# Trace of a batched matrix product: from casting loads with transposed B and a VectorE multiply-reduce to plain float32 loads with transposed A and TensorE matmuls

## The chip, the cores and the metric

The kernel runs on 1 core of one Trainium2 chip. Its time is the device time of one execution in microseconds (us). The span of a profile is some 2 us shorter than that time (718.2 against 720.2 us for the kernel before), because it covers the program's instructions alone. Ratios are computed as the mean time of one kernel's fast runs over that of the other's fast runs of the same rounds, so they are not quite the ratios of the medians quoted beside them.

## The reference

Eight pairs of 2176 x 2176 float32 matrices come in, eight numbers go out:

```python
def reference(a, b):                       # a, b: (8, 2176, 2176) float32
    prod = np.matmul(a, b)
    traces = np.diagonal(prod, axis1=1, axis2=2).sum(axis=-1)
    return traces.astype(np.float32)
```

Only the diagonal of each product is needed, so each trace is the sum over i and k of A[i,k] * B[k,i]. Each input number is used once. One of the two matrices must be transposed on the chip, so that A[i,k] and B[k,i] meet. (HBM is the memory that the inputs lie in, SBUF the memory on the chip that the engines read, PSUM the one that TensorE writes its results to; DMA engines carry the data from HBM to SBUF.) In this text a row tile is 128 rows of one matrix, 128 x 2176 numbers, 1.114 MB in float32. There are 17 in a matrix and 272 in all, 303.04 MB.

## The kernel before

The loads go through GpSimd and cast float32 to bf16 on the way. A whole A matrix lies in SBUF, double-buffered. Rows of B arrive in groups of two, their 128 x 128 blocks are transposed on TensorE into PSUM, and VectorE multiplies them with the matching part of A and sums.

```python
    a_pool = ctx.enter_context(tc.tile_pool(name="a_pool", bufs=2))
    b_pool = ctx.enter_context(tc.tile_pool(name="b_pool", bufs=5))
    # ... cut ...
    def load(dst, src, start, m):
        rows = src[start:start + P * m, :].rearrange("(p r) k -> p r k", r=m)
        nc.gpsimd.dma_start(out=dst, in_=rows)          # float32 -> bf16 on the way
    # ... cut: for each batch, for each group of B's rows ...
            load(b_tile[:, 0:m, :], b[bi], start, m)
            if not last:
                load_a(a_next, bi + 1, gi)
            for lo, hi in chunks:                        # 6, 6 and 5 blocks
                for s in range(m):
                    psum_tile = psum_pool.tile([P, 6, P], dt, tag="bT")
                    for u in range(lo, hi):
                        c0, step = slot_cols[u]
                        nc.tensor.transpose(
                            psum_tile[:, u - lo, :],
                            b_tile[:, s, c0:c0 + step * (P - 1) + 1:step],
                            identity,
                        )
                    nc.vector.tensor_tensor_reduce(      # product with A, and its sum
                        out=scratch[:, :w, :],
                        in0=a_all[:, lo:hi, start + s:start + s + m * (P - 1) + 1:m],
                        in1=psum_tile[:, :w, :],
                        # ... cut: multiply, add ...
                        accum_out=acc[:, col:col + 1],
                    )
```

Of the kernel before, what the change touches and what calls it, by code (L numbers as in the profile page):

```python
# [1 line left out]

# [5 lines left out]


def row_groups(n, p, rows):  # L10

    groups, at = [], 0
    while at < n:
        m = min(rows, (n - at) // p)
        groups.append((at, m))
        at += m * p
    return groups


@with_exitstack  # L20
def kernel(
    ctx: ExitStack,
    tc: tile.TileContext,
    a: bass.AP,
    b: bass.AP,
    out: bass.AP,
):
    nc = tc.nc
    P = 128
    BATCH, N, N2 = a.shape  # L30
    assert N == N2 and N % P == 0
    NT = N // P
    ROWS = 2
    CHUNKS = [(0, 6), (6, 12), (12, NT)]
    LAST_CHUNKS = [(0, 6), (6, 12), (12, 16), (16, NT)]

    dt = mybir.dt.bfloat16
    f32 = mybir.dt.float32

    const = ctx.enter_context(tc.tile_pool(name="const", bufs=1))  # L40
    a_pool = ctx.enter_context(tc.tile_pool(name="a_pool", bufs=2))
    b_pool = ctx.enter_context(tc.tile_pool(name="b_pool", bufs=5))
    psum_pool = ctx.enter_context(tc.tile_pool(name="psum", bufs=7, space=bass.MemoryType.PSUM))
    psum_small = ctx.enter_context(tc.tile_pool(name="psum_small", bufs=1, space=bass.MemoryType.PSUM))
    scratch_pool = ctx.enter_context(tc.tile_pool(name="scratch", bufs=2))
    acc_pool = ctx.enter_context(tc.tile_pool(name="acc", bufs=2))

    groups = row_groups(N, P, ROWS)

    slot_cols = [(start + r, m) for start, m in groups for r in range(m)]  # L50

    def load(dst, src, start, m):
        rows = src[start:start + P * m, :].rearrange("(p r) k -> p r k", r=m)
        nc.gpsimd.dma_start(out=dst, in_=rows)  # L54

    def load_a(a_all, bi, gi):
        start, m = groups[gi]
        slot = start // P
        load(a_all[:, slot:slot + m, :], a[bi], start, m)

    a_next = a_pool.tile([P, NT, N], dt, tag="a")
    for gi in range(len(groups)):
        load_a(a_next, 0, gi)

    identity = const.tile([P, P], dt, tag="identity")
    make_identity(nc, identity)
    ones = const.tile([P, 1], f32, tag="ones")
    nc.vector.memset(ones, 1.0)  # L68
    batch_accs = const.tile([P, BATCH], f32, tag="batch_accs")
    result_tile = const.tile([P, BATCH], f32, tag="result")  # L70

    for bi in range(BATCH):
        a_all = a_next
        last = bi == BATCH - 1
        b_groups = row_groups(N, P, 1 if last else ROWS)
        acc = acc_pool.tile([P, NT * len(LAST_CHUNKS)], f32, tag="acc")
        col = 0
        if not last:
            a_next = a_pool.tile([P, NT, N], dt, tag="a")

        for gi, (start, m) in enumerate(b_groups):
            b_tile = b_pool.tile([P, ROWS, N], dt, tag="b")
            pieces = last and gi >= len(b_groups) - 2
            chunks = LAST_CHUNKS if pieces else CHUNKS
            if pieces:
                for lo, hi in chunks:
                    nc.gpsimd.dma_start(  # L87
                        out=b_tile[:, 0, lo * P:hi * P],
                        in_=b[bi, start:start + P, lo * P:hi * P],
                    )  # L90
            else:
                load(b_tile[:, 0:m, :], b[bi], start, m)

            if not last:
                load_a(a_next, bi + 1, gi)

            for lo, hi in chunks:
                for s in range(m):
                    w = hi - lo
                    psum_tile = psum_pool.tile([P, 6, P], dt, tag="bT")  # L100
                    for u in range(lo, hi):
                        c0, step = slot_cols[u]
                        nc.tensor.transpose(  # L103
                            psum_tile[:, u - lo, :],
                            b_tile[:, s, c0:c0 + step * (P - 1) + 1:step],
                            identity,
                        )
                    scratch = scratch_pool.tile([P, 6, P], dt, tag="scr")
                    nc.vector.tensor_tensor_reduce(  # L109
                        out=scratch[:, :w, :],  # L110
                        in0=a_all[:, lo:hi, start + s:start + s + m * (P - 1) + 1:m],
                        in1=psum_tile[:, :w, :],
                        scale=1.0,
                        scalar=0.0,
                        op0=mybir.AluOpType.mult,
                        op1=mybir.AluOpType.add,
                        accum_out=acc[:, col:col + 1],
                    )
                    col += 1

        nc.vector.reduce_sum(  # L121
            out=batch_accs[:, bi:bi + 1], in_=acc[:, :col], axis=mybir.AxisListType.X
        )

    batch_psum = psum_small.tile([1, BATCH], f32, tag="bp")
    nc.tensor.matmul(batch_psum, ones, batch_accs, start=True, stop=True)  # L126
    nc.vector.tensor_copy(out=result_tile[:1, :BATCH], in_=batch_psum)  # L127

    nc.sync.dma_start(
        out=out.rearrange("(a b) -> a b", a=1),  # L130
        in_=result_tile[:1, :BATCH],
    )


# [1 line left out]
_INS = ['a', 'b']  # L136
_OUTS = [((8,), 'float32')]


# [23 lines left out]
```

## Time and profile before

| | before |
|---|---|
| time, median | 720.2 us |
| span of the profile | 718.2 us |
| read from HBM | 303.04 MB |
| load queue's share of the 16 DMA engines' span | 101.4% |
| VectorE, TensorE matmuls busy | 48%, 35% |
| instruction packets on the DMA engines | 18 |

The page of the profile before says first what each engine did. In the strips, each of 40 columns is one slice of the span, with the busy share in tenths or the GB/s that the DMA engines wrote. PE is TensorE's matmuls, PEld its weight loads, DVE VectorE, ACT ScalarE, POOL GpSimd, and SP SyncE. Then come the DMA queues with their packets, MB and share of the engines, and the chain of waits that ended last.

```profile
span 718.2 us, 6176 instructions
PE 248.2 (35%) x2314; PEld 228.3 (32%) x2314; DVE 347.1 (48%) x830; POOL 84.6 (12%) x164
...
DMA  8999999999999999999999999999999999999995
...
q0 software_dynamic: 22752, 151.53, 101.4%
q8 instruction: 18, 0.29, 0.1%
...
DMA 93%; issue 3%; PE 2%; DVE 1%; POOL 0%; POOLq 0%; ACTq 0%
```

The DMA engines are busy for 90% or more of every slice but the first and the last, and 93% of the chain is DMA. No compute engine is busy for half the span.

The table by stage for the kernel before gives, for each stretch of time, the busy us of each engine, the granted TensorE clock (as a share of full speed), the DMA share and the GB/s written:

```profile
core 0: us, PE busy (x) PEld busy (x) DVE busy (x) POOL busy (x), PEclk, DMA share, GB/s
20.00:600.00 580.00, 194.69 (x1802) 181.09 (x1802) 269.99 (x642) 62.58 (x118) 0.63 1.03 216
...
690.00:712.00 22.00, 13.56 (x151) 11.24 (x149) 21.74 (x51) 5.83 (x11) 0.78 0.95 180
```

bf16 is written and float32 is read, so 216 GB/s written are about 430 GB/s read. In the tail (the last line) VectorE is busy for 21.74 of 22 us, so there it is VectorE that ends last, on a backlog.

Two lines of the timeline before (start, us, engine, line, operation, tiles, how often, and the idle time before with its releaser) serve for the pace of TensorE: 34 transposes take 3.81 us.

```profile
646.84 3.54 PEld L103 LDWEIGHTS <-b_tile 128*128 128x128 bf16 x34 [6.79 <-DMA b_tile<-in_b_dram]
646.84 3.81 PE L103 MATMUL psum_tile<-identity,b_tile 128*128 128x128 bf16 x34 [6.53 <-DMA b_tile<-in_b_dram]
```

### The profile page before, as it was taken

What the parts mean: (1) busy time and instruction counts of PE and PEld (TensorE: products, weight loads), DVE (VectorE), ACT (ScalarE), POOL (GpSimd) and SP (SyncE); (2) the same over time, 40 slices, a digit from 0 to 9 for tenths busy, and PEclk for the clock granted to TensorE, in tenths of its full rate; (3) what the DMA queues carried; (4) which work ended last, traced back from release to release, by engine and by line L of the source; (5) the groups of instructions that cost most, each with busy time, mean ns of one, the idle gap of its engine ahead of it and who ended that gap; (6) DMA issues with size and microseconds to landing.
All of it is one profiled execution on the core that took longest, in us unless ns stands there. A gap on an engine that the chain in (4) does not pass through costs nothing.

```text
span 718.2 us, 6176 instructions
## 1 busy us (share of the span) xinstructions
PE 248.2 (35%) x2314; PEld 228.3 (32%) x2314; DVE 347.1 (48%) x830; POOL 84.6 (12%) x164
## 2 busy tenths in 40 slices
PE   0004422324424244342343332444323442324664
PEld 0003322323323133332333332333223331323553
DVE  0005445455445455454554544545435553445798
POOL 3011010201002010021010210102010020100121
PEclk9998666566665656655555555665555565555567
DMA  8999999999999999999999999999999999999995
GB/s 177 215 214 216 216 217 215 214 217 216 216 216 215 215 216 216 215 216 215 216 215 214 216 216 216 215 214 217 216 215 215 214 218 216 214 216 214 213 214 100
DMA packets 22784, 151.92 MB, mean 212 GB/s; under 512 B 2786, under 2 KB 3554, under 8 KB 7394
## 3 DMA queue, kind: packets, MB, share of 16 engines
q0 software_dynamic: 22752, 151.53, 101.4%
q8 instruction: 18, 0.29, 0.1%
q14 instruction: 12, 0.10, 0.0%
q1 hardware_dynamic: 2, 0.00, 0.0%
HBM read 303.04 MB, written 0.00 MB: 422 GB/s over the span
## 4 chain that ended last, share of the span: by engine, by line
DMA 93%; issue 3%; PE 2%; DVE 1%; POOL 0%; POOLq 0%; ACTq 0%
DMA b_tile<-in_b_dram 86%; DMA a_next<-in_a_dram 7%; PE psum_tile L103 2%; DVE scratch L109 1%; POOL a_next L54 0%; DVE acc L109 0%; DVE batch_accs L121 0%; POOLq L54 0%; PE batch_psum L126 0%; DVE result_tile L127 0%; ACTq L158 0%
## 5 line engine op out<-in xcount | busy, mean ns | idle before, releaser
L109 DVE CUSTOM_DVE_ANT_0 scratch<-a_next,psum_tile 128x768 bf16<-128x768 bf16 (+1 forms) x410 | 344.7, 903 | 367.8 <-PE psum_tile L103 367.0
L103 PE MATMUL psum_tile<-identity,b_tile 128*128 128x128 bf16 x2312 | 248.0, 302 | 465.5 <-DMA b_tile<-in_b_dram 459.4
L103 PEld LDWEIGHTS <-b_tile 128*128 128x128 bf16 x2312 | 228.2, 143 | 485.1 <-DMA b_tile<-in_b_dram 485.1
L54 POOL DMA_DIRECT2D a_next<-in_a_dram x72 | 38.7, 542 | 329.3 <-DVE batch_accs L121 157.1
L54 POOL DMA_DIRECT2D b_tile<-in_b_dram x78 | 41.7, 535 | 286.1 <-DMA b_tile<-in_b_dram 151.0
L109 DVE DVE_READ_ACCUMULATOR2_ANT acc<- 128x1 f32 x410 | 34.0, 83 | 0.0
L87 POOL DMA_DIRECT2D b_tile<-in_b_dram x8 | 4.2, 537 | 7.6 <-DMA b_tile<-in_b_dram 4.1
L121 DVE TENSOR_REDUCE batch_accs<-acc 128x1 f32<-128x51 f32 (+1 forms) x8 | 1.7, 206 | 0.3
L126 PE MATMUL batch_psum<-batch_accs,ones 128*1 128x8 f32 x2 | 0.2, 173 | 2.4 <-DVE batch_accs L121 2.4
L126 PEld LDWEIGHTS batch_psum<-batch_accs,ones 128*1 128x1 f32 x2 | 0.1, 80 | 2.6 <-DVE batch_accs L121 2.6
L68 DVE MEMSET ones<- 128x1 f32 x1 | 0.1, 59 | 0.8 <-PEq L147 0.8
masks.py:199 POOL TENSOR_SCALAR_AFFINE_SELECT identity<-identity 128x128 bf16<-128x128 bf16 x1 | 0.3, 307 | 0.1
L127 DVE COPY result_tile<-batch_psum 1x8 f32<-1x8 f32 x1 | 0.2, 153 | 0.3 <-PE batch_psum L126 0.3
masks.py:197 POOL MEMSET identity<- 128x128 bf16 x1 | 0.2, 229 | 0.0
L147 POOL MEMSET const-float32-0.0<- 128x1 f32 x1 | 0.1, 99 | 0.2 <-issue 0.2
L147 POOL MEMSET const-bfloat16-1.0<- 128x1 bf16 x1 | 0.1, 102 | 0.0
L147 POOL MEMSET const-uint8-127<- 128x1 uint8 x1 | 0.1, 102 | 0.0
L147 POOL MEMSET const-float32-1.0<- 128x1 f32 x1 | 0.1, 99 | 0.0
## 6 DMA issues: line engine op xcount, KB each, us to landing
a_next<-in_a_dram POOLq DMA_DIRECT2D x64, 1088.0 KB, 38.5
b_tile<-in_b_dram POOLq DMA_DIRECT2D x56, 1088.0 KB, 38.5
b_tile<-in_b_dram POOLq DMA_DIRECT2D x22, 544.0 KB, 15.5
a_next<-in_a_dram POOLq DMA_DIRECT2D x8, 544.0 KB, 36.2
b_tile<-in_b_dram POOLq DMA_DIRECT2D x4, 192.0 KB, 10.0
b_tile<-in_b_dram POOLq DMA_DIRECT2D x2, 128.0 KB, 9.1
b_tile<-in_b_dram POOLq DMA_DIRECT2D x2, 32.0 KB, 7.7
out_dram<-result_tile SPq DMA_DIRECT2D x1, 0.0 KB
```

The source lines that it names most:

```text
L54: nc.gpsimd.dma_start(out=dst, in_=rows)
L68: nc.vector.memset(ones, 1.0)
L87: nc.gpsimd.dma_start(out=b_tile[:, 0, lo * P:hi * P], in_=b[bi, start:start + P, lo * P:hi * P],)
L103: nc.tensor.transpose(psum_tile[:, u - lo, :], b_tile[:, s, c0:c0 + step * (P - 1) + 1:step], identity,)
L109: nc.vector.tensor_tensor_reduce(out=scratch[:, :w, :], in0=a_all[:, lo:hi, start + s:start + s + m * (P - 1) + 1:m], in1=psum_tile[:, :w, :],
L121: nc.vector.reduce_sum(out=batch_accs[:, bi:bi + 1], in_=acc[:, :col], axis=mybir.AxisListType.X)
L126: nc.tensor.matmul(batch_psum, ones, batch_accs, start=True, stop=True)
L127: nc.vector.tensor_copy(out=result_tile[:1, :BATCH], in_=batch_psum)
L147: nc = _bacc.Bacc("TRN2", target_bir_lowering=False, num_devices=1)
```

## The change

Intent: let the loads be plain float32 copies issued from SyncE, in larger pieces (four rows per partition), and move the work from VectorE to TensorE. In the A stage of each batch, VectorE rounds A's row tiles to bf16, TensorE transposes the blocks, and ScalarE copies them out of PSUM into one SBUF tile `at`. In the B stage, VectorE and ScalarE in turn round B's row tiles, and TensorE multiplies the blocks, summing all 289 products of a batch into one 128 x 128 PSUM tile. Its diagonal is summed once per batch.

```diff
-    ROWS = 2
+    ROWS = 4
+    even = [ROWS] * (NT // ROWS) + [1] * (NT % ROWS)
+    fine = [4, 4, 4, 1, 1, 1, 1, 1]                    # B of the last batch
...
+    at_pool = ctx.enter_context(tc.tile_pool(name="at_pool", bufs=1))
+    stage = ctx.enter_context(tc.tile_pool(name="stage", bufs=3))
+    cast_pool = ctx.enter_context(tc.tile_pool(name="cast", bufs=3))
...
+    def load(src, start, m):
+        t = stage.tile([P, ROWS, N], f32, tag="stage")
+        rows = src[start:start + P * m, :].rearrange("(p r) k -> p r k", r=m)
+        nc.sync.dma_start(out=t[:, 0:m, :], in_=rows)
+        return t
...
+        at = at_pool.tile([P, NT, NT, P], dt, tag="at")
+        for start, m in a_groups:                       # A stage
+            a_t = load(a[bi], start, m)
+            for r in range(m):
+                a_c = cast_pool.tile([P, N], dt, tag="cast")
+                nc.vector.tensor_copy(out=a_c, in_=a_t[:, r, :])
+                for v0 in range(0, NT, 6):
+                    ...                                 # up to 6 transposes into ps
+                    nc.scalar.copy(out=at[:, v0:v1, u0 + r, :], in_=ps[:, 0:v1 - v0, :])
+        trace_ps = psum_acc.tile([P, P], f32, tag="trace")
+        for gi, (start, m) in enumerate(b_groups):      # B stage
+            ...                                         # load, the last row tile in four pieces
+            for s in range(m):
+                b_c = cast_pool.tile([P, N], dt, tag="cast")
+                ...                                     # nc.scalar.copy or nc.vector.tensor_copy
+                for u in range(NT):
+                    c0, step = u_cols[u]
+                    nc.tensor.matmul(
+                        trace_ps,
+                        at[:, v0 + s, u, :],                       # stationary
+                        b_c[:, c0:c0 + step * (P - 1) + 1:step],   # moving, step 4
+                        start=..., stop=...,
+                    )
```

A partition gets four neighbouring rows of a matrix, so a 128-wide block is picked with a step of 4 elements.

More of the change, by code (lines that the diff above doesn't have):

```diff
@@ L7, with row_groups @@
 from concourse._compat import with_exitstack
-def row_groups(n, p, rows):
+def row_groups(p, rows):
     groups, at = [], 0
-    while at < n:
-        m = min(rows, (n - at) // p)
+    for m in rows:
         groups.append((at, m))
@@ L32 @@
     NT = N // P
-    ROWS = 2
-    CHUNKS = [(0, 6), (6, 12), (12, NT)]
-    LAST_CHUNKS = [(0, 6), (6, 12), (12, 16), (16, NT)]
+    ROWS = 4
     dt = mybir.dt.bfloat16
     f32 = mybir.dt.float32
-    const = ctx.enter_context(tc.tile_pool(name="const", bufs=1))
-    a_pool = ctx.enter_context(tc.tile_pool(name="a_pool", bufs=2))
-    b_pool = ctx.enter_context(tc.tile_pool(name="b_pool", bufs=5))
-    psum_pool = ctx.enter_context(tc.tile_pool(name="psum", bufs=7, space=bass.MemoryType.PSUM))
@@ L44 @@
-    psum_small = ctx.enter_context(tc.tile_pool(name="psum_small", bufs=1, space=bass.MemoryType.PSUM))
-    scratch_pool = ctx.enter_context(tc.tile_pool(name="scratch", bufs=2))
-    acc_pool = ctx.enter_context(tc.tile_pool(name="acc", bufs=2))
-    groups = row_groups(N, P, ROWS)
-    slot_cols = [(start + r, m) for start, m in groups for r in range(m)]
-    def load(dst, src, start, m):
-        rows = src[start:start + P * m, :].rearrange("(p r) k -> p r k", r=m)
-        nc.gpsimd.dma_start(out=dst, in_=rows)
@@ L56, in load_a @@
-    def load_a(a_all, bi, gi):
-        start, m = groups[gi]
-        slot = start // P
-        load(a_all[:, slot:slot + m, :], a[bi], start, m)
-    a_next = a_pool.tile([P, NT, N], dt, tag="a")
-    for gi in range(len(groups)):
-        load_a(a_next, 0, gi)
-    identity = const.tile([P, P], dt, tag="identity")
-    make_identity(nc, identity)
-    ones = const.tile([P, 1], f32, tag="ones")
-    nc.vector.memset(ones, 1.0)
-    batch_accs = const.tile([P, BATCH], f32, tag="batch_accs")
-    result_tile = const.tile([P, BATCH], f32, tag="result")
+    even = [ROWS] * (NT // ROWS) + [1] * (NT % ROWS)
@@ new lines @@
+    fine = [4, 4, 4, 1, 1, 1, 1, 1]
+    assert sum(even) == NT and sum(fine) == NT
+    a_groups = row_groups(P, even)
+    u_cols = [(start + r, m) for start, m in a_groups for r in range(m)]
+    LAST_PIECES = [(0, 8), (8, 12), (12, 16), (16, NT)]
+    const = ctx.enter_context(tc.tile_pool(name="const", bufs=1))
+    at_pool = ctx.enter_context(tc.tile_pool(name="at_pool", bufs=1))
+    stage = ctx.enter_context(tc.tile_pool(name="stage", bufs=3))
+    cast_pool = ctx.enter_context(tc.tile_pool(name="cast", bufs=3))
@@ new lines @@
+    psum_pool = ctx.enter_context(tc.tile_pool(name="psum", bufs=5, space=bass.MemoryType.PSUM))
+    psum_acc = ctx.enter_context(tc.tile_pool(name="psum_acc", bufs=2, space=bass.MemoryType.PSUM))
+    psum_small = ctx.enter_context(tc.tile_pool(name="psum_small", bufs=1, space=bass.MemoryType.PSUM))
+    def load(src, start, m):
+        t = stage.tile([P, ROWS, N], f32, tag="stage")
+        rows = src[start:start + P * m, :].rearrange("(p r) k -> p r k", r=m)
+        nc.sync.dma_start(out=t[:, 0:m, :], in_=rows)
+        return t
@@ L72 @@
+    identity = None
+    evac = 0
     for bi in range(BATCH):
-        a_all = a_next
         last = bi == BATCH - 1
-        b_groups = row_groups(N, P, 1 if last else ROWS)
-        acc = acc_pool.tile([P, NT * len(LAST_CHUNKS)], f32, tag="acc")
-        col = 0
-        if not last:
-            a_next = a_pool.tile([P, NT, N], dt, tag="a")
-        for gi, (start, m) in enumerate(b_groups):
-            b_tile = b_pool.tile([P, ROWS, N], dt, tag="b")
-            pieces = last and gi >= len(b_groups) - 2
-            chunks = LAST_CHUNKS if pieces else CHUNKS
-            if pieces:
-                for lo, hi in chunks:
-                    nc.gpsimd.dma_start(
-                        out=b_tile[:, 0, lo * P:hi * P],
+        b_groups = row_groups(P, fine if last else even)
+        v_cols = [(start + s, m) for start, m in b_groups for s in range(m)]
+        at = at_pool.tile([P, NT, NT, P], dt, tag="at")
+        for start, m in a_groups:
+            a_t = load(a[bi], start, m)
+            if identity is None:
+                identity = const.tile([P, P], dt, tag="identity")
+                make_identity(nc, identity)
+                ones = const.tile([P, 1], f32, tag="ones")
+                nc.vector.memset(ones, 1.0)
+                batch_accs = const.tile([P, BATCH], f32, tag="batch_accs")
+                result_tile = const.tile([P, BATCH], f32, tag="result")
+                masked = const.tile([P, P], f32, tag="masked")
+            u0 = start // P
+            for r in range(m):
+                a_c = cast_pool.tile([P, N], dt, tag="cast")
+                nc.vector.tensor_copy(out=a_c, in_=a_t[:, r, :])
+                for v0 in range(0, NT, 6):
+                    v1 = min(v0 + 6, NT)
+                    ps = psum_pool.tile([P, 6, P], dt, tag="aT")
+                    for v in range(v0, v1):
+                        c0, step = v_cols[v]
+                        nc.tensor.transpose(
+                            ps[:, v - v0, :],
+                            a_c[:, c0:c0 + step * (P - 1) + 1:step],
+                            identity,
+                        )
+                    nc.scalar.copy(out=at[:, v0:v1, u0 + r, :], in_=ps[:, 0:v1 - v0, :])
+        trace_ps = psum_acc.tile([P, P], f32, tag="trace")
+        for gi, (start, m) in enumerate(b_groups):
+            if last and gi == len(b_groups) - 1:
+                b_t = stage.tile([P, ROWS, N], f32, tag="stage")
+                for lo, hi in LAST_PIECES:
+                    nc.sync.dma_start(
+                        out=b_t[:, 0, lo * P:hi * P],
@@ L91 @@
             else:
-                load(b_tile[:, 0:m, :], b[bi], start, m)
-            if not last:
-                load_a(a_next, bi + 1, gi)
-            for lo, hi in chunks:
-                for s in range(m):
-                    w = hi - lo
-                    psum_tile = psum_pool.tile([P, 6, P], dt, tag="bT")
-                    for u in range(lo, hi):
-                        c0, step = slot_cols[u]
-                        nc.tensor.transpose(
-                            psum_tile[:, u - lo, :],
-                            b_tile[:, s, c0:c0 + step * (P - 1) + 1:step],
-                            identity,
-                        )
-                    scratch = scratch_pool.tile([P, 6, P], dt, tag="scr")
-                    nc.vector.tensor_tensor_reduce(
-                        out=scratch[:, :w, :],
-                        in0=a_all[:, lo:hi, start + s:start + s + m * (P - 1) + 1:m],
-                        in1=psum_tile[:, :w, :],
-                        scale=1.0,
-                        scalar=0.0,
-                        op0=mybir.AluOpType.mult,
-                        op1=mybir.AluOpType.add,
-                        accum_out=acc[:, col:col + 1],
-                    )
-                    col += 1
@@ L121 @@
-        nc.vector.reduce_sum(
-            out=batch_accs[:, bi:bi + 1], in_=acc[:, :col], axis=mybir.AxisListType.X
+                b_t = load(b[bi], start, m)
+            v0 = start // P
+            for s in range(m):
+                b_c = cast_pool.tile([P, N], dt, tag="cast")
+                for lo, hi in LAST_PIECES if last and gi >= len(b_groups) - 2 else [(0, NT)]:
+                    cut = slice(lo * P, hi * P)
+                    if evac % 2 == 0:
+                        nc.scalar.copy(out=b_c[:, cut], in_=b_t[:, s, cut])
+                    else:
+                        nc.vector.tensor_copy(out=b_c[:, cut], in_=b_t[:, s, cut])
+                    evac += 1
+                for u in range(NT):
[4 more added lines that the diff above has]
+                        b_c[:, c0:c0 + step * (P - 1) + 1:step],
+                        start=(v0 + s == 0 and u == 0),
+                        stop=(v0 + s == NT - 1 and u == NT - 1),
+                    )
@@ L123 @@
+        nc.vector.tensor_tensor_reduce(
+            out=masked,
+            in0=identity,
+            in1=trace_ps,
+            scale=1.0,
+            scalar=0.0,
+            op0=mybir.AluOpType.mult,
+            op1=mybir.AluOpType.add,
+            accum_out=batch_accs[:, bi:bi + 1],
         )
```

## The prediction

> **What bounds the kernel now.** The DMA engines. The page of before puts 93% of the chain that ended last on DMA (86% b_tile, 7% a_next), the DMA row reads 9 in 38 of 40 slices, and the queue table charges the load queue 101.4% of the 16 engines' span. HBM reads are 303.04 MB, 422 GB/s over the 718.2 us span. In the stage table the stretches between 20 and 600 us write 215 to 216 GB/s of bf16, that is 430 to 432 GB/s of float32 read; at that rate the inputs alone need about 703 us. What is left is a head (first bytes at about 3 us) and a tail: the DMA rate drops at about 709 us, and VectorE works on to 716 us. VectorE is 48% busy, PE 35%.
>
> **What the change removes, adds and moves.** The 303 MB read stay; written to SBUF are now 303 MB instead of 151.5, the cast leaving the DMA. The 410 VectorE multiply-reduces (344.7 us) and their accumulator reads go. Per 128x2176 row tile (2.585 us of DMA at 431 GB/s) come:
> - A stage: a VectorE round[...]; 17 transposes, 2.0 us (17 took 2.01 us in the timeline of before, 34 took 3.82); three ScalarE evictions. ScalarE does nothing in before[...].
> - B stage: a round, alternately VectorE[...] and ScalarE[...], and 17 matmuls of 128 columns, at most 2.0 us.
>
> **On the critical path.** Every engine stays below 2.585 us per row tile[...]. The single A-transposed buffer makes next batch's evictions wait for the last matmul of this one, but three stage buffers of up to 4 row tiles (10.3 us of DMA each) let loads run on; rounding frees a buffer about 6 us after landing, before the following load has ended. So I expect DMA still to end the waits, with no gap at batch boundaries. PE's work doubles, to some 500 us in all: off the path.
>
> Small terms: the head is about 1 us shorter; in the last batch the single-row loads wait for stage buffers held by the last 4-row load, perhaps 2 us of DMA gap; the tail after the last landing is 5 us instead of 7.
>
> **Rate.** The open point is whether the plain load keeps 431 GB/s with twice the SBUF write. [...]before's read side already runs at 431, its write side never above 216. I take 428 to 431.
>
> **Sum.** 704 (data) + 2 (head) + 2 (gap) + 5 (tail) + 2 (outside the span, as 720.2 against 718.2) = about 716 us. Range 706 to 735.
>
> **Chances.** Faster by over 2%: 0.09. Within 2%: 0.77. Slower by over 2%: 0.14.
>
> **What would show it.** DMA row near 9 throughout with some 430 GB/s written; chain mostly DMA stage; [...]PE 65 to 75%; no DMA dips every 88 us[...].
>
> **What would make it wrong.** Plain writes capped below 420 GB/s (slower); ScalarE evictions over 0.9 us, which would make the A stage ScalarE-bound and starve the loads; PE pace over 150 ns with stride-4 operands (17 would then take 2.55 us); DMA dips at each boundary because the buffers free in groups of four rows.

The sum adds to 704 + 2 + 2 + 5 + 2 = 715, quoted as "about 716". The 704 us are 303.04 MB at 430.5 GB/s, inside the 430 to 432 read off the kernel before; the gap and the tail are estimates. The profile after: rounding took 1.29 us on VectorE and 2.005 us on ScalarE, three evictions 0.861 + 0.861 + 0.772 = 2.49 us, and 17 matmuls at 116 ns 1.97 us. It also has the other times named there: a buffer of four row tiles came free 4.9 us (A) or 5.5 us (B) after its first rounding had begun, and the first data packet started at 1.76 us against 2.60 us in the kernel before. The write side "never above 216" is meant by stage; single slices of the page's strip read up to 218.

## The result, and the profile after

The time after is 725.36 us (724.49 to 725.75, 4 runs) against 720.23 us: ratio 1.0070, 95% interval 1.0052 to 1.0087. That lies within the 2% called "same" and inside the predicted range of 706 to 735 us, but 9.4 us above the predicted 716, and on the other side of the time before.

The page after:

```profile
span 723.5 us, 10432 instructions
PE 484.9 (67%) x4626; PEld 471.1 (65%) x4626; DVE 256.3 (35%) x225; ACT 412.7 (57%) x480; POOL 0.7 (0%) x6
...
DMA  9999999999999999999999999999999999999985
...
q1 hardware_dynamic: 12386, 303.04, 98.2%
q8 instruction: 36, 0.59, 0.3%
...
DMA 79%; DVE 9%; PE 7%; ACT 2%; issue 2%; DVEq 0%; ACTq 0%; SPq 0%
```

DMA still fills the span, except in the last slices. VectorE is down to 35%, ScalarE is at 57% and TensorE at 67% (65 to 75% was predicted). The instruction packets of q8 have doubled from 18 to 36.

The groups of instructions after, each kind of shape by itself (count, then busy us and the mean ns of one):

```profile
L121 PE MATMUL trace_ps<-b_c,at 128*128 128x128 bf16 x2312 | 267.2, 293 | 101.7 <-ACT b_c L115 52.4 <-DVE b_c L117 49.3
...
L96 ACT COPY at<-ps 128x768 bf16<-128x768 bf16 x272 | 211.9, 861 | 128.5 <-PE ps L91 128.5
L85 DVE CAST a_c<-t 128x2176 bf16<-128x2176 f32 x136 | 167.2, 1289 | 157.3 <-DMA t<-in_a_dram 154.8
L115 ACT CAST b_c<-t 128x2176 bf16<-128x2176 f32 x67 | 132.8, 2005 | 171.6 <-DMA t<-in_b_dram 137.8 <-PE trace_ps L121 33.8
```

The two lines of rounding (L85, L115) idle mostly for DMA, and the DMA share of the middle is 1.00 in the next table: there the engines wait for loads, not the loads for engines.

The table by stage after, the middle and the tail:

```profile
20.00:600.00 580.00, 394.70 (x3781) 383.93 (x3779) 210.63 (x180) 342.60 (x406) 0.00 (x0) 0.74 1.00 429
...
702.30:709.00 6.70, 6.61 (x59) 6.61 (x59) 2.53 (x3) 3.35 (x3) 0.00 (x0) 0.61 0.38 122
709.00:715.00 6.00, 6.00 (x56) 5.98 (x54) 1.29 (x1) 1.38 (x1) 0.00 (x0) 1.00 0.98 372
715.00:724.00 9.00, 5.26 (x46) 4.74 (x43) 1.67 (x7) 3.13 (x4) 0.00 (x0) 0.81 0.23 87
```

(The columns are PE, PEld, VectorE, ScalarE, GpSimd, clock, DMA share, GB/s.) Two things differ from the prediction. In the tail the DMA rate falls to 122 GB/s for 6.7 us, while TensorE is busy for 6.61 of 6.7 and for all of the next 6 us. And the steady rate is 429 GB/s, about what I had assumed, yet the last 4-row load was ready only at 701.0 us. By the packet records 4.25 MB of the inputs were still to come then, against 2.01 MB at the same time in the plain loads by themselves (below). Even in the version below that closes the gap the last data packet ended at 713.8 us, where I had counted on 706 us.

The timeline after shows the tail itself:

```profile
701.04 2.50 DVE L117 CAST b_c<-t 128x2176 bf16<-128x2176 f32 x2 [7.85 <-DMA t<-in_b_dram]
702.39 13.61 PE L121 MATMUL trace_ps<-b_c,at 128*128 128x128 bf16 x119 [2.48 <-DVE b_c L117]
...
704.54 2.01 ACT L115 CAST b_c<-t 128x2176 bf16<-128x2176 f32 x1 [1.52 <-PE trace_ps L121]
706.54 1.29 DVE L117 CAST b_c<-t 128x2176 bf16<-128x2176 f32 x1 [3.00 <-ACT b_c L115]
...
716.62 4.07 PE L121 MATMUL trace_ps<-b_c,at 128*128 128x128 bf16 x34 [0.63 <-ACT b_c L115]
```

From 702.39 us on TensorE does 153 matmuls, nine row tiles, in 18.3 us and idles for only 0.63 us of it. Its pace is 13.61 us / 119 = 114 ns each, although the granted clock is 1.00 between 709 and 715 us. The fourth rounding of the last 4-row load has to wait for TensorE (for a free `b_c`), so its load buffer comes free only at 706.55 us, and the third single-row load, which takes this buffer, is issued then (the first two had been issued by 696.2 us). That is the DMA gap.

So there were two questions. In the tail, is it the gap in the loads or the pace of TensorE that costs? And why was the stream of loads late at 701 us?

### The profile page after: what moved, and what is told of

The parts are those of the page before. It is cut to its first block, busy times and chain, and to the rows that moved or that the text cites. A ratio compares the mean times of both kernels' runs of the same rounds, so it can differ in the third digit from the quotient of the medians.

```text
span 723.5 us, 10432 instructions
## 1 busy us (share of the span) xinstructions
PE 484.9 (67%) x4626; PEld 471.1 (65%) x4626; DVE 256.3 (35%) x225; ACT 412.7 (57%) x480; POOL 0.7 (0%) x6
## 3 DMA queue, kind: packets, MB, share of 16 engines
q1 hardware_dynamic: 12386, 303.04, 98.2%
HBM read 303.04 MB, written 0.00 MB: 419 GB/s over the span
## 4 chain that ended last, share of the span: by engine, by line
DMA 79%; DVE 9%; PE 7%; ACT 2%; issue 2%; DVEq 0%; ACTq 0%; SPq 0%
DMA t<-in_a_dram 48%; DMA t<-in_b_dram 31%; DVE a_c L85 7%; PE ps L91 4%; PE trace_ps L121 3%; ACT b_c L115 2%; DVE b_c L117 2%; DVEq L85 0%; DVE masked L129 0%; DVEq L117 0%; PE batch_psum L141 0%; ACTq L115 0%; DVE result_tile L142 0%; SPq L57 0%; DVE batch_accs L129 0%
## 5 line engine op out<-in xcount | busy, mean ns | idle before, releaser
L96 ACT COPY at<-ps 128x768 bf16<-128x768 bf16 (+1 forms) x408 | 275.4, 831 | 128.5 <-PE ps L91 128.5
L121 PE MATMUL trace_ps<-b_c,at 128*128 128x128 bf16 x2312 | 267.2, 293 | 101.7 <-ACT b_c L115 52.4
L121 PEld LDWEIGHTS <-at 128*128 128x128 bf16 x2312 | 262.7, 120 | 106.0 <-issue 105.6
L91 PE MATMUL ps<-identity,a_c 128*128 128x128 bf16 x2312 | 217.6, 280 | 134.3 <-DVE a_c L85 129.8
L91 PEld LDWEIGHTS <-a_c 128*128 128x128 bf16 x2312 | 208.6, 136 | 143.5 <-DVE a_c L85 135.6
L115 ACT CAST b_c<-t 128x2176 bf16<-128x2176 f32 (+1 forms) x69 | 134.4, 1970 | 176.8 <-DMA t<-in_b_dram 143.0
L85 DVE CAST a_c<-t 128x2176 bf16<-128x2176 f32 x136 | 167.2, 1289 | 157.3 <-DMA t<-in_a_dram 154.8
L117 DVE CAST b_c<-t 128x2176 bf16<-128x2176 f32 (+1 forms) x69 | 85.9, 1264 | 264.4 <-DMA t<-in_b_dram 204.9
L129 DVE CUSTOM_DVE_ANT_0 masked<-identity,trace_ps 128x128 f32<-128x128 bf16 x8 | 2.3, 287 | 40.1 <-PE trace_ps L121 40.1
L115 ACT CAST b_c<-b_t 128x1024 bf16<-128x1024 f32 (+1 forms) x2 | 1.7, 830 | 0.6 <-DMA b_t<-in_b_dram 0.6
## 6 DMA issues: line engine op xcount, KB each, us to landing
t<-in_a_dram SPq DMA_DIRECT2D x8, 1088.0 KB, 18.3
```

The costliest lines, as they stand in the source:

```text
L85: nc.vector.tensor_copy(out=a_c, in_=a_t[:, r, :])
L91: nc.tensor.transpose(ps[:, v - v0, :], a_c[:, c0:c0 + step * (P - 1) + 1:step], identity,)
L96: nc.scalar.copy(out=at[:, v0:v1, u0 + r, :], in_=ps[:, 0:v1 - v0, :])
L115: nc.scalar.copy(out=b_c[:, cut], in_=b_t[:, s, cut])
L117: nc.vector.tensor_copy(out=b_c[:, cut], in_=b_t[:, s, cut])
L121: nc.tensor.matmul(trace_ps, at[:, v0 + s, u, :], b_c[:, c0:c0 + step * (P - 1) + 1:step], start=(v0 + s == 0 and u == 0), stop=(v0 + s == ...
```

## The experiments

Eight kernels ran, all with three rounds.

### Matmul operands exchanged

```diff
                     nc.tensor.matmul(
                         trace_ps,
-                        at[:, v0 + s, u, :],
-                        b_c[:, c0:c0 + step * (P - 1) + 1:step],
+                        b_c[:, c0:c0 + step * (P - 1) + 1:step],
+                        at[:, v0 + s, u, :],
```

> The two operands of the 2312 B-stage matmuls change places: the stride-4 slices of the rounded B row become the stationary operand, the contiguous A-transposed block the moving one (the result is the transposed block, its diagonal the same). Theory S (the stride of the moving operand sets the 116 ns pace, whatever the clock): the start-to-start pace falls to what the transposes show, 107 ns at half clock and 56 ns at full clock; the nine last row tiles no longer take 18.3 us of PE; the last loads are issued earlier; time about 720 us (5 us less than the change's 725.4). Rival A (accumulating into one PSUM bank sets the pace): it stays at 116 ns and the time at 725.

Measured: correct, 724.96 us (724.42 to 725.22), ratio to before 1.0064 (1.0047 to 1.0080). The pace did what theory S says. The same four row tiles, 68 matmuls, in the timelines of both kernels, first the change, then the exchanged operands:

```profile
603.31 7.87 PE L121 MATMUL trace_ps<-b_c,at 128*128 128x128 bf16 x68 [2.47 <-ACT b_c L115]
```

```profile
603.39 5.62 PE L121 MATMUL trace_ps<-at,b_c 128*128 128x128 bf16 x68 [4.33 <-ACT b_c L115]
```

The granted clock differed in this stretch (0.71 against 0.82 from 600 to 612 us), so the distances at equal clock decide. Over the whole run, the median distance from one matmul's start to the next, taken from the trace's start times, is 116 ns at both granted clocks in the change. With the operands exchanged it is 107 ns at clock 0.5 and 56 ns at clock 1.0, as for the transposes. Both kernels accumulate into one PSUM tile, so rival A, the accumulation, falls. What is shown is that a moving operand with a step of 4 elements (8 bytes) costs the pace, and the same slice as stationary operand does not.

But the time hardly moved: my expected 5 us did not come. The table by stage for this kernel, for the same stretches as above, says why:

```profile
702.30:709.00 6.70, 6.69 (x82) 6.69 (x83) 2.45 (x2) 4.19 (x3) 0.00 (x0) 0.67 0.41 139
709.00:715.00 6.00, 2.88 (x40) 2.27 (x38) 1.29 (x1) 0.48 (x1) 0.00 (x0) 0.88 0.99 393
```

The gap in the loads is still there (139 GB/s), and TensorE now waits for them: it is busy for 2.88 of 6 us where it had been busy for all 6. The fourth rounding ran from 704.35 to 706.36 us, almost as in the change: at the half clock the first row's 17 matmuls took about 17 x 107 ns = 1.8 us, little less than before, and the rounding on ScalarE takes 2.0 us after that.

### The last single rows in buffers that are already free

```diff
+            row = 0
+            if last and m == 1:
+                row = singles % ROWS
+                if row == 0:
+                    b_t = stage.tile([P, ROWS, N], f32, tag="stage")
+                singles += 1
+                ...            # nc.sync.dma_start into b_t[:, row, :]; the last row in its pieces
...
-                        nc.scalar.copy(out=b_c[:, cut], in_=b_t[:, s, cut])
+                        nc.scalar.copy(out=b_c[:, cut], in_=b_t[:, row + s, cut])
```

Four of the five single rows share one stage buffer and the last has another. Both are free long before.

> The last batch's single-row loads share stage buffers (four rows in one, the last row in another), which are free by then, so they need not wait for the roundings of the last 4-row load. PE untouched. Theory P (the tail is bound by PE: nine row tiles of matmuls at 2.0 us behind the last 4-row landing, PE idle there only 0.6 us): the DMA gap of about 5 us at 703 to 708 us goes, but the time falls by 1 us at most, to 724.5 or above. Rival G (the DMA gap in the tail is on the critical path): the time falls by the gap, 4 to 6 us, to 720.

Measured: correct, 724.48 us (724.30 to 724.58), ratio to before 1.0059 (1.0044 to 1.0074). The gap is gone and the median time is 0.9 us lower. The table by stage and, after it, the timeline of this kernel:

```profile
702.30:709.00 6.70, 6.67 (x59) 6.66 (x59) 2.48 (x2) 3.38 (x3) 0.00 (x0) 0.75 1.00 409
709.00:715.00 6.00, 6.00 (x56) 5.98 (x55) 2.42 (x5) 3.79 (x4) 0.00 (x0) 1.00 0.31 119
```

```profile
702.33 17.41 PE L126 MATMUL trace_ps<-b_c,at 128*128 128x128 bf16 x153 [2.48 <-DVE b_c L122]
```

The loads run at 409 GB/s through the stretch in which they had run at 122, and are over before 715 us. TensorE does all 153 matmuls without a break in 17.41 us, 114 ns each, and still ends at 719.7 us. Theory P holds for this kernel: with the slow pace, the gap cost at most the 0.9 us. Rival G falls as a cause on its own.

### Both edits

> Both edits. Theory S with P: PE at 56 to 107 ns follows the single rows as they land and the loads have no gap, so the last landing is at about 714 us and the end some 4 us later: time 718 to 719.5 us, less than either edit alone. Rival A with P: 724.5. Rival G: 720, as pack alone.

Measured: correct, 719.97 us (719.69 to 720.00), ratio to before 0.9995 (0.9981 to 1.0010). Its table by stage:

```profile
702.30:709.00 6.70, 6.50 (x79) 6.51 (x80) 2.63 (x3) 4.16 (x3) 0.00 (x0) 0.65 0.96 392
709.00:715.00 6.00, 4.51 (x74) 3.99 (x72) 2.51 (x5) 3.83 (x5) 0.00 (x0) 1.00 0.32 124
715.00:724.00 9.00, 0.61 (x10) 0.33 (x7) 0.45 (x3) 0.00 (x0) 0.00 (x0) 0.83 0.00 0
```

The median falls by 0.4 us with one edit alone, by 0.9 us with the other alone, and by 5.4 us with both (725.36 - 719.97). The first two are not clear of the spread of the change's own runs (724.49 to 725.75 us); the third is. The tail had two limits side by side, the loads' gap and TensorE's pace, and the later of the two ends it. Taking either away leaves the other standing at nearly the same place. My expectation of 718 to 719.5 us was slightly too low; the direction and the size of the step held. This is the best version that came out, and it only equals the kernel before.

### The plain loads by themselves

The body is replaced by the same loads (in even groups in the last batch too), each followed by one small VectorE copy. Its output is wrong, which doesn't matter for the time.

```diff
+    for bi in range(BATCH):
+        for x in (a, b):
+            for start, m in a_groups:
+                t = load(x[bi], start, m)
+                nc.vector.tensor_copy(out=seen[:, 0:1], in_=t[:, m - 1, N - 1:N])
```

> Wrong result on purpose: only the change's loads (4-row plain float32 loads from SyncE, three buffers), each read by one tiny VectorE copy. It measures what the loads cost by themselves. Theory L (the 0.3% lower steady rate of the change, 428.5 against 430 GB/s read, lies in the plain loads themselves): 428 to 429 GB/s again, span about 711 us, time about 713. Rival C (the compute engines' traffic slows the loads): over 430 GB/s, time 708 to 711 us.

Measured: 709.93 us (709.82 to 710.17), ratio to before 0.9857 (0.9843 to 0.9872). The table by stage:

```profile
20.00:600.00 580.00, 10.15 (x66) 0.00 (x0) 1.00 1.00 431
```

The last data packet ended at 706.9 us (from the packet records of the trace). That is the 706 us on which the prediction had counted. Plain loads with twice the SBUF write are not slower (431 GB/s, against about 430 GB/s read in the kernel before); theory L falls. Something in the rest of the program makes the change's loads late. My rival C named the data traffic of the compute engines, but the page showed another difference: no instruction packets on q8 here, 36 in the change. The next two runs tell these apart.

### Loads beside TensorE instructions, and loads beside rounding

To the plain loads, the first kernel adds as many TensorE instructions as the change has, on one small operand; the second adds the rounding of all row tiles and nothing on TensorE. Their outputs are wrong, which doesn't matter for the times. They were run on another chip.

```diff
+                w = w_pool.tile([P, P], dt, tag="w")
+                nc.vector.tensor_copy(out=w, in_=t[:, m - 1, N - P:N])
+                for r in range(m):
+                    ps = psum_pool.tile([P, P], f32, tag="ps")
+                    for u in range(NT):
+                        nc.tensor.matmul(ps, w, w, start=(u == 0), stop=(u == NT - 1))
```

> Wrong result on purpose: the plain loads alone, plus 17 matmuls per loaded row tile on PE (4624 weight loads and 4624 matmuls, as many as in the change), all on one small 128x128 operand, so hardly any further data moves. Theory I (what slows the change's loads against loads alone, 428.5 against 431.1 GB/s, is the fetching of instructions over the same DMA engines: 36 packets of mostly 16 KB, about 1 us each, none in loads alone): some 35 such packets again, the read rate falls to 428 to 429 GB/s and the time rises from 709.9 to 713 to 716 us. Rival C (data traffic of the compute engines in SBUF): the time stays within 1.5 us of 709.9 plus the longer tail of a few matmuls, that is below 712.

```diff
+                for r in range(m):
+                    c = cast_pool.tile([P, N], dt, tag="cast")
+                    if x is b and evac % 2 == 0:
+                        nc.scalar.copy(out=c, in_=t[:, r, :])
+                    else:
+                        nc.vector.tensor_copy(out=c, in_=t[:, r, :])
+                    evac += 1
```

> Wrong result on purpose: the plain loads alone, plus the rounding of all 272 row tiles to bf16 on VectorE and ScalarE as in the change, without PE work. Few instructions, but 303 MB read from and 151 MB written to SBUF by the compute engines. Theory I: hardly any instruction packets, rate 431 GB/s, time 710 to 713 us (a few us for the rounding of the last row tile). Rival C: the rate falls to 428 to 429 GB/s and the time rises to 715 or more.

Measured: with the TensorE instructions 720.42 us (719.91 to 721.33), ratio to before 1.0004 (0.9989 to 1.0019); with the rounding 711.55 us (711.15 to 711.65), ratio 0.9880 (0.9864 to 0.9897). So TensorE instructions that load nothing more from HBM cost 10.5 us over the loads alone (part of it is the matmuls left after the last landings). Rounding all 303 MB costs 1.6 us, and its last data packet ended at 706.7 us, as in the loads alone. Rival C falls, and theory I's direction holds; the time is above the 713 to 716 us that I had expected. The queue table with TensorE instructions has the same instruction packets as the change, and its tail shows what they do:

```profile
q8 instruction: 36, 0.59, 0.3%
```

```profile
704.00:706.00 2.00, 2.00 (x34) 2.00 (x32) 0.00 (x0) 0.00 (x0) 0.87 0.76 322
706.00:708.00 2.00, 0.19 (x4) 0.02 (x1) 0.00 (x0) 0.00 (x0) 1.00 0.48 209
708.00:710.00 2.00, 0.00 (x0) 0.00 (x0) 0.00 (x0) 0.00 (x0) 1.00 0.39 165
710.00:712.00 2.00, 1.10 (x15) 1.11 (x16) 0.23 (x1) 0.00 (x0) 0.84 0.38 157
```

The loads do not slow evenly. Up to 706 us the rate is nearly that of the loads alone (430 against 431 GB/s from 20 to 600 us, 396 against 405 from 700 to 704 us). From then to 712 us the engines' mean busy share is 0.48 to 0.38. The packet records count it out: 16 data packets are in flight at 704.5 us and 8 from 706.5 to 710.5 us, so half of the engines have finished and the other half are still at work. The last data packet ended at 712.6 us instead of 706.9.

A load reports its landing in 16 parts, and the next step waits for the last of them. From the first to the last part the last 4-row load took 1.6 us in the loads alone, but 8.0 us here (1.0 us for the first load of the run), and 5.5 us in the change, where the parts came from 695.5 to 700.9 us and the rounding began at 701.0. So the mean rate (429 or 430 GB/s) hides most of the delay, which grows through the run.

The records also show what one instruction packet does. It takes 1.06 us on average, and while it is in flight 15.05 data packets are, against 16.04 otherwise (20 to 690 us): it takes the place of one data packet. If the 36 packets are spread over eight engines, that is 36 x 1.06 / 8 = 4.8 us for each engine, an estimate from these numbers, against the measured delay of 5.7 us. That the packets fall on just the eight late engines is inferred; the records do not name the engine.

### Half and twice the TensorE instructions

The kernel with TensorE instructions again, with 8 matmuls per row tile, then with 34 small ones of 32 x 32.

```diff
-                    for u in range(NT):
-                        nc.tensor.matmul(ps, w, w, start=(u == 0), stop=(u == NT - 1))
+                    for u in range(8):
+                        nc.tensor.matmul(ps, w, w, start=(u == 0), stop=(u == 7))
```

> Wrong result on purpose: as the run with 17 matmuls per row tile beside the plain loads, with 8 instead. Theory I (instruction fetching delays half of the DMA engines): about half the instruction packets (17 of 36), so the stretch at half the DMA rate at the end, 6 us long with 17 matmuls, is about 3 us long, and the time about 714 us. Rival W (it is PE's activity or the wait for the last matmuls, not the fetches): no half-rate stretch tied to the number of fetches.

```diff
-                    for u in range(NT):
-                        nc.tensor.matmul(ps, w, w, start=(u == 0), stop=(u == NT - 1))
+                    for u in range(34):
+                        nc.tensor.matmul(ps[:32, :32], w[:, :32], w[:, :32],
+                                         start=(u == 0), stop=(u == 33))
```

> Wrong result on purpose: as the run with 17 matmuls per row tile, with 34 small ones of 32x32 instead: twice the instructions, less PE array work each. Theory I: about 72 instruction packets, the slower half of the DMA engines some 11 to 12 us behind, so a half-rate stretch of that length at the end, or where three buffers do not allow so much lag, a lower rate before it; time 725 to 730 us. Rival W: no more delay than with 17 matmuls, time 720 or less.

| run | TensorE instructions | instruction packets | end of the last data packet, us | time, us | ratio to before (95%) |
|---|---|---|---|---|---|
| loads alone | none | 0 | 706.9 | 709.93 | 0.9857 (0.9843 to 0.9872) |
| 8 matmuls per row tile | 4352 | 17 | 709.7 | 714.73 | 0.9921 (0.9907 to 0.9936) |
| 17 matmuls per row tile | 9248 | 36 | 712.6 | 720.42 | 1.0004 (0.9989 to 1.0019) |
| 34 small matmuls per row tile | 18496 | 72 | 719.6 | 725.08 | 1.0068 (1.0052 to 1.0085) |

(A matmul is two instructions, a weight load and the matmul.) The queue tables of the last kernel and, after it, of the first show the packets:

```profile
q8 instruction: 72, 1.18, 0.7%
```

```profile
q8 instruction: 17, 0.28, 0.2%
```

The end of the loads moves by 2.8, 5.7 and 12.6 us for 17, 36 and 72 packets: 0.16 to 0.18 us for each. The last kernel has less work per matmul in the array (TensorE was busy for 10.34 us between 690 and 720 us, against 17.74 us with 17 matmuls) and by its shapes reads half as much of SBUF for them, yet has twice the delay. It is the number of instructions that counts, and rival W falls. The times rise by 2 to 5 us more than the ends of the loads do, because in these kernels the matmuls of the last two loads still follow the landings; the fourth column is therefore the one to compare.

## Why the prediction was right or wrong

**Right: what bounds the kernel, and the class.** DMA still fills the span; 79% of the chain is DMA. The time is within 2% and within the range. The direction inside that class was wrong: 0.6% faster was predicted, 0.7% slower was measured. The plain load keeps the rate: 431 GB/s by itself, as the mean over 580 us (single slices of the page's strip read up to 450 GB/s).

**Right: the middle of the run.** No engine starved the loads between batches: the DMA share was 1.00 from 20 to 600 us. PE was predicted at 65 to 75% and was at 67%; VectorE was at 35% and ScalarE at 57%. The rounding took 1.29 us on VectorE and 2.005 us on ScalarE. An eviction took 0.861 us for 768 columns and 0.772 us for 640, so that three of them, about 2.5 us, still fit under the 2.585 us of DMA per row tile.

Two steps of the prediction failed: the end of the loads, "704 (data) + 2 (head)", and what follows it, "2 (gap) + 5 (tail)" with TensorE "off the path".

**Wrong: "704 (data) + 2 (head)".** For loads alone it is right: they end at 706.9 us. But the sum left out the instruction stream. The change's 9252 TensorE instructions come in over the same DMA engines in 36 packets, twice as many as before, and 36 such packets moved the end of the loads by 5.7 us in the run that added only TensorE instructions to the loads. I had read the mean rate of the kernel before, 430 GB/s, and a mean cannot show that some engines run behind. (The landing parts show it in the kernel before too: those of one load came over 1.9 us at the start and over 6.3 us near the end, in a tail that was bound by VectorE.) The mechanism "DMA-bound at an unchanged rate" stands for data; the missed term is one of traffic. That it costs the same 5.7 us inside the change is carried over from the run with the same number of packets; the instructions could not be taken out of the change itself. The two versions without the gap, with 36 packets too, ended their loads at 713.8 and 714.0 us, 7 us after the loads alone. So the delay is there in full kernels, and some 1.3 us of it is not accounted for. (Their packets of 34,816 bytes took 1.298 us on average, against 1.296 us with the TensorE instructions and 1.295 us alone; why is open.)

**Wrong: "PE's work doubles ... off the path" and "2 (gap) + 5 (tail)".** Per row tile, 17 matmuls took 17 x 116 ns = 1.97 us, as predicted ("at most 2.0 us"), and under 2.585 us that is off the path in the steady state. In the tail it is not. A 4-row load hands over four row tiles at once, and five more can follow in 13 us (they had landed by 714.2 us in the version without the gap), so TensorE has 9 x 2 us to do behind the landing at 701 us. The gap was also larger than 2 us: the rate was 122 GB/s over 6.7 us, against 409 with free buffers, which is 4.7 us of loading lost. The two lay beside each other, and from the end of loads with that instruction traffic (712.6 us) to the end of the span (723.5 us) there were 10.9 us in place of 7, so 3.9 us too few in the prediction. The two edits that remove both limits took 5.4 us off.

**The sum.** The terms of the text add to 715, quoted as "about 716": a span of 713. The measured span is 723.5, which is 713 + 0.9 (loads alone, 706.9 for 706) + 5.7 (instruction packets) + 3.9 (tail). The last term is what remains, not an independent measurement. The version with both edits gives the same total from full kernels alone: its loads ended at 714.0 us, 8.0 later than predicted, and 4.2 us followed, 2.8 less than predicted, which makes its span of 718.2; the gap and the pace together add the 5.3 us up to 723.5.

**The warning that did not come true.** The prediction feared a pace over 150 ns with step-4 operands. The pace was affected, 116 ns whatever the clock, just not beyond what I had costed at the lower clock. What was missed was that it would not get better when the clock rose.

**Open.** Why only half of the DMA engines are delayed is not settled. Of the 0.16 us per packet, the packet's own time spread over eight engines gives 0.13 (an estimate, 1.06 / 8); whether the rest is an uneven spread or something else is open. What ended the loads of the kernel before at 712.9 us, with only 18 instruction packets, was not tested. As moving operand, no kernel tried another step in place of 4.

## What to carry to other kernels

In a kernel that is bound by DMA, as this one, the instructions of an unrolled program can be DMA traffic that counts (36 packets, 5.7 us): count them, compare the instruction queue's packets before and after, and look at how evenly the engines finish, since a load here was ready only when the slowest had done its part (the parts of the change's last 4-row load came from 695.5 to 700.9 us, and its rounding began at 701.0). When a tail has two limits side by side, taking away one can show next to nothing (0.4 and 0.9 us here, against 5.4 us for both); try both together before either is called harmless. Where a matmul's operands can be exchanged (here only the diagonal mattered), try the strided slice as the stationary one and the contiguous block as the moving one; for bf16 with a step of 4 that took the pace from 116 ns to 56 ns at the full clock.
